# A transformer block, a state-space layer and an attention layer on one core: the transpositions between two stages moved half a block of products

## The chip, the cores and the metric

The kernel runs on one core of a Trainium2 chip. Its time is device microseconds from the start to the end of one execution. Five engines work side by side, each through its own list of instructions in a fixed order: TensorE (PE, matrix products and transpositions), VectorE (DVE), ScalarE (ACT), GpSimd (POOL) and SyncE (SP, which issues the DMAs). An instruction waits until what it reads is written, and everything behind it on its engine waits with it.

## The reference

512 tokens of width 1024 in 32-bit floats go through four stages. Each stage norms its input, scales and shifts it by vectors that come from a condition c, computes, and adds its output to the running x.

```python
def first_block(x, c, ...):
    sh1, sc1, g1, sh2, sc2, g2 = split(silu(c) @ ada_w + ada_b, 6)
    h = rms_norm(x, mix_pre_g) * (1 + sc1) + sh1
    y = hybrid_mixer(h, ...)                    # forgetting attention beside a convolution, then @ w_o
    x = x + g1 * rms_norm(y, mix_post_g)
    h = rms_norm(x, ffn_pre_g) * (1 + sc2) + sh2
    y = swiglu_ffn(h, w_ffn_in, w_ffn_out)      # silu(h @ Wg) * (h @ Wu) @ w_ffn_out
    return x + g2 * rms_norm(y, ffn_post_g)

def second_block(x, c_2, ...):
    x = x + gate * _mamba2_mixer(_modulate(x, norm_g[0], shift, scale), ...)   # ends in @ m_out_w
    kv = _modulate(x, kv_norm_g, kv_shift, kv_scale) @ kv_w
    x = x + gate * _sb_mixer(_modulate(x, norm_g[1], shift, scale), k, v, ...) # ends in @ sb_out_w
    return _rmsnorm(x, final_g)
```

## The kernel before

The 512 tokens are four blocks of 128. Every product of two 32-bit matrices is made of three products of a faster format (`mm3`, L328 to L330): each operand is split into a high part, a cast, and a low part, the rest. For weights ACT casts the high part (`whi`, L269) and DVE or POOL subtracts (`wlo`, L273). A ring of four `whi`/`wlo` buffers holds split weights, and four `raw` buffers hold what DMAs have brought; a raw buffer is loaded again when its weight is split. Some weights that are needed early go into buffers named `b` instead of the ring. Between the splits DVE also sums condition vectors from further weights that pass through the same raw buffers (L503, L505).

Three times one stage ends and the next begins: I call these places the joins. The first lies between the attention and the feed-forward part, the second between that and the mamba mixer, the third between mamba and the last attention. All three are written by `boundary`, which goes through a table of steps, `BOUNDARY`; a step is a letter and a block of tokens:

- m: the last products of the block with the output weights of the ending stage, into two PSUM buffers of 512 columns (`Out.last`, L328 to L330). For blocks 2 and 3 these are 24 products, 12 for each half of the columns.
- a: squares of the sums on ACT (L574; none at the third join) and the gate on DVE (L632)
- b, d, n: the inverse root of the mean square, six tiny instructions that alternate between DVE and ACT (L581 to L586); n does d of one block and b of the next
- c: the sum goes to x on DVE (L642; L644 at the third join), squares of x on ACT (L574)
- e: x scaled by the root into `w`: the first half on DVE (L656), the second on ACT (L658)
- r: the eight transpositions on PE, four from each half (L664), into `pa` buffers for blocks 0 and 1, `ps` buffers for blocks 2 and 3
- f: scale and shift, the first half on DVE (L674 x4), the second on ACT (L676 x4), then the high part of both halves on ACT (L680) and the low part on POOL (L681). At the third join also copies of the transposed block (L684).
- p: the first products of the next stage with that block (24 of them, L328 to L330), which read the high and low parts
- l: what comes after p (an activation or a copy out of PSUM)

The table is not the order in which an engine works. It is the order of writing; a scheduler orders each engine's instructions by their readiness as it estimates it and by a priority, which `PRIO` gives each letter (`bm` is not in it, `bp` -200, `br` -5, with other numbers in some stages). So moving a step in the table moves instructions on every engine that has to do with it.

Of the kernel before, what the change touches and what calls it, by code (L numbers as in the profile page):

```python
# [50 lines left out]
AHEAD = 11  # L51


BOUNDARY = ("m0 a0 b0 m1 m2 a1 c0 n0 e0 c1 a2 r0 n1 f0 e1 r1 m3 c2 a3 n2 p0 e2 f1 c3 n3 e3 r2 l0 f2 p1 l1 r3 p2 "
            "l2 f3 p3 l3")


class Unit:
# [71 lines left out]
class Body:  # L130
# [557 lines left out]
    def boundary(self, out, gate, norm, mod, h, first, keep=None):  # L688

        nc = self.nc  # L690
        st = [self.block(t, lambda t=t: out.pss[t], gate, norm, mod, h, keep) for t in range(NT)]
        nc.scalar.activation(self.small(), self.ones[:, 0:1], AF.Sqrt, scale=0.0)
        for s in BOUNDARY.split():
            kind, t = s[0], int(s[1])
            with self.prio("b" + kind):
                if kind == "m":
                    self.run(out.last(t))
                elif kind == "p":
                    self.run(first[t])
                elif kind == "n":  # L700

                    self.side(st[t]["d"]() if t >= 0 else [], st[t + 1]["b"]() if t + 1 < NT else [])
                elif kind == "b":
                    self.side(st[t]["b"]())
                elif kind == "d":
                    self.side(st[t]["d"]())
                elif kind == "l":
                    self.late.pop(0)()
                else:
                    st[t][kind]()  # L710
# [1019 lines left out]
```

## Time and profile before

| what | value |
|---|---|
| median of 3 runs | 1388.56 us (1387.05 to 1390.49) |
| the profiled execution's own time | 1386.6 us |
| its span, first to last instruction | 1384.9 us |
| PE busy with products | 1315.4 us, 95% of the span, 7477 instructions |
| DVE, ACT, POOL busy | 877.3 us (63%), 661.4 us (48%), 313.6 us (23%) |
| granted clock of PE, mean | 0.987 of full speed |

The profile is of one execution. Times within it count from the span's start. A row of the timeline gives the start of a group of equal instructions and how long they were busy; products are pipelined, so the steps between their starts tell their cost, not the time beside them. A number in square brackets is idle time of the engine just before, and what ended it.

### The profile page before, as it was taken

The page shows a single profiled execution, that of the slowest core. Times are in us where ns is not written, and L with a number is a line of the kernel's source. Part 1 is how long each engine was busy: PE and PEld are TensorE (multiplying, and loading weights), DVE is VectorE, ACT ScalarE, POOL GpSimd, SP SyncE. Part 2 cuts the span into 40 slices and gives each one's busy share as a digit, 9 for nine tenths or more (in the row PEclk, how much of TensorE's full clock was granted, in tenths as well). Part 3 has the DMA queues.
Part 4 walks back from the last instruction along what each step waited for, and adds up shares of the span by engine and source line. Part 5 has one row for each costly group of instructions (what it writes and reads, how often), then busy time and mean ns, then how long its engine had stood idle before and what let it go on. Part 6 is the DMA issues. An engine that isn't in the chain of part 4 may idle for free. (4 is left out here: it accounts for less than half of the span.)

```text
span 1384.9 us, 19700 instructions
## 1 busy us (share of the span) xinstructions
PE 1315.4 (95%) x7477; PEld 1024.8 (74%) x7479; DVE 877.3 (63%) x1267; ACT 661.4 (48%) x1214; POOL 313.6 (23%) x322
## 2 busy tenths in 40 slices
PE   7899899999999999999999999999899999999997
PEld 5574566777888888888768777777688787777766
DVE  7924676465455443622868889767744966777865
ACT  4433248355222223412667566667542835555543
POOL 3541323023000000000111434342400412433421
PEclk9999899999999999999999999999999999999999
DMA  9668664205376554223167455414024354232211
GB/s 301 171 181 240 184 184 136 61 16 174 115 235 213 195 187 159 91 91 111 46 183 253 137 169 162 152 52 160 32 91 137 107 168 122 76 94 75 96 42 61
DMA packets 134731, 189.06 MB, mean 137 GB/s; under 512 B 10280, under 2 KB 95556, under 8 KB 133612
## 3 DMA queue, kind: packets, MB, share of 16 engines
q1 hardware_dynamic: 134588, 187.79, 43.9%
q8 instruction: 59, 0.97, 0.3%
q14 instruction: 36, 0.29, 0.1%
q10 hardware_dynamic: 48, 0.01, 0.0%
HBM read 178.25 MB, written 3.24 MB: 131 GB/s over the span
## 5 line engine op out<-in xcount | busy, mean ns | idle before, releaser
L273 DVE TENSOR_TENSOR wlo<-raw,whi 128x1024 fp32r<-128x1024 f32 (+1 forms) x160 | 209.6, 1321 | 204.8 <-ACT whi L269 194.7
L269 ACT CAST whi<-raw 128x1024 fp32r<-128x1024 f32 (+1 forms) x177 | 182.8, 1045 | 285.9 <-PE pa L329 121.0
L329 PE MATMUL pa<-b,whi 128*128 128x512 f32 x744 | 298.6, 401 | 0.0
L328 PE MATMUL pa<-b,whi 128*128 128x512 f32 x744 | 298.4, 401 | 0.0
L330 PE MATMUL pa<-b,wlo 128*128 128x512 f32 x744 | 297.5, 400 | 0.0
L329 PE MATMUL pa<-wlo,b 128*128 128x512 f32 x424 | 167.1, 394 | 1.9 <-DVE sm L581 1.9
L328 PE MATMUL pa<-whi,b 128*128 128x512 f32 x424 | 166.4, 394 | 1.9 <-ACT b L90 1.5
L330 PE MATMUL pa<-whi,b 128*128 128x512 f32 x424 | 166.3, 394 | 0.0
L330 PEld LDWEIGHTS pa<-b,wlo 128*128 128x128 f32 x744 | 140.7, 189 | 31.9 <-issue 2.1
L505 DVE SCALAR_TENSOR_TENSOR acc<-raw,c,acc 128x1024 f32<-128x1024 f32 x84 | 118.5, 1411 | 71.6 <-DMA raw<-in_ada_w_dram 46.5
L328 PEld LDWEIGHTS pa<-b,whi 128*128 128x128 f32 x744 | 140.6, 189 | 31.3 <-issue 4.9
L329 PEld LDWEIGHTS pa<-b,whi 128*128 128x128 f32 x744 | 140.7, 189 | 29.6 <-issue 0.8
L681 POOL TENSOR_TENSOR b<-w,b 128x512 fp32r<-128x512 f32 x24 | 36.7, 1546 | 469.1 <-DVE sm L586 288.0
L328 PEld LDWEIGHTS pa<-whi,b 128*128 128x128 f32 x424 | 80.0, 189 | 19.4 <-issue 1.8
L329 PEld LDWEIGHTS pa<-wlo,b 128*128 128x128 f32 x424 | 79.9, 188 | 19.4 <-DVE wlo L273 2.7
L330 PEld LDWEIGHTS pa<-whi,b 128*128 128x128 f32 x424 | 79.9, 189 | 17.3 <-issue 0.6
L1452 DVE TENSOR_TENSOR_SCAN w<-w,own 128x512 f32<-128x512 f32 (+3 forms) x64 | 64.1, 1046 | 15.2 <-ACT w L1449 15.2
L1454 POOL TENSOR_TENSOR w<-w,w 128x511 f32<-128x511 f32 (+3 forms) x64 | 67.7, 1063 | 22.1 <-DVE w L1452 21.2
L328 PE MATMUL ps<-whi,b 128*128 128x512 f32 x184 | 72.3, 393 | 0.0
L329 PE MATMUL ps<-wlo,b 128*128 128x512 f32 x184 | 72.1, 392 | 0.0
L330 PE MATMUL ps<-whi,b 128*128 128x512 f32 x184 | 72.0, 391 | 0.0
L273 POOL TENSOR_TENSOR wlo<-raw,whi 128x1024 fp32r<-128x1024 f32 (+1 forms) x17 | 41.3, 2432 | 72.9 <-ACT whi L269 65.9
(356 smaller groups left out, 2179.7 us busy)
## 6 DMA issues: line engine op xcount, KB each, us to landing
raw<-in_ada_w_dram SPq DMA_DIRECT2D x80, 512.0 KB
raw<-in_w_ffn_in_dram SPq DMA_DIRECT2D x44, 512.0 KB
raw<-in_m_in_w_dram SPq DMA_DIRECT2D x40, 512.0 KB
raw<-in_w_ffn_out_dram SPq DMA_DIRECT2D x22, 512.0 KB
b<-in_ada_w_dram SPq DMA_DIRECT2D x16, 512.0 KB
raw<-in_kv_ada_w_dram SPq DMA_DIRECT2D x16, 512.0 KB
b<-cumd SPq DMA_DIRECT2D x8, 1024.0 KB
raw<-in_m_out_w_dram SPq DMA_DIRECT2D x16, 512.0 KB
```

The source lines that it names most:

```text
L269: nc.scalar.copy(hi[:, :n], u.raw)
L273: eng.tensor_tensor(lo[:, :n], u.raw, hi[:, :n].bitcast(F32), ALU.subtract)
L328: mm(ps, lhsT=lh, rhs=rh, start=first, stop=False)
L329: mm(ps, lhsT=lh, rhs=rl, start=False, stop=False)
L330: mm(ps, lhsT=ll, rhs=rh, start=False, stop=last)
L505: nc.vector.scalar_tensor_tensor(acc, raw, ck, acc, ALU.mult, ALU.add)
L681: nc.gpsimd.tensor_tensor(lo, y[i], hi.bitcast(F32), ALU.subtract)
L1452: nc.vector.tensor_tensor_scan(R[:, 0:N][:, ::-1], R[:, 0:N][:, ::-1], self.own[:, S - N : S][:, ::-1], 0.0, ALU.mult, ALU.max)
L1454: nc.gpsimd.tensor_tensor(pr_[:, : N - 1], pr_[:, : N - 1], R[:, 1:N], ALU.mult)
```

## The change

The table gets two new letters. h is the first half of an m step's products (the first 512 columns), q the first half of a p step's; a later m or p of the same block does what is left. Block 0's transpositions r0 stood before all of block 3's last products m3 and now stand behind their first half (h3); r1 stood before m3 and now stands behind it; r2 stood before p1 and now stands behind its first half (q1). r3 stays. The function keeps the list of products that is left of a block.

```diff
-BOUNDARY = ("m0 a0 b0 m1 m2 a1 c0 n0 e0 c1 a2 r0 n1 f0 e1 r1 m3 c2 a3 n2 p0 e2 f1 c3 n3 e3 r2 l0 f2 p1 l1 r3 p2 "
-            "l2 f3 p3 l3")
+BOUNDARY = ("m0 a0 b0 m1 m2 a1 c0 n0 e0 c1 a2 h3 r0 n1 f0 e1 m3 r1 c2 a3 n2 p0 e2 f1 c3 n3 e3 q1 r2 l0 f2 p1 l1 r3 "
+            "p2 l2 f3 p3 l3")
...
+        last = {}
         for s in BOUNDARY.split():
             kind, t = s[0], int(s[1])
-            with self.prio("b" + kind):
-                if kind == "m":
-                    self.run(out.last(t))
-                elif kind == "p":
-                    self.run(first[t])
+            with self.prio("b" + {"h": "m", "q": "p"}.get(kind, kind)):
+                if kind in "hm":
+                    if t not in last:
+                        last[t] = out.last(t)
+                    l = last[t]
+                    self.run([l.pop(0) for _ in range(len(l) // 2 if kind == "h" else len(l))])
+                elif kind in "qp":
+                    l = first[t]
+                    self.run([l.pop(0) for _ in range(len(l) // 2 if kind == "q" else len(l))])
```

Three places show what the scheduler makes of it. On PE at the third join, the kernel before has the last of block 0's first products (into `pa_9281`), then one product of block 1 (`pa_9380`), then the transpositions of block 2 (from `w_9312` and `w_9314`):

```order
L330 MATMUL pa_9281<-whi_9234,b_9060 128x512
L328 MATMUL pa_9380<-b_9024,b_9057 128x512
L664 MATMUL ps_9354<-ident,w_9312 128x128 x4
L664 MATMUL ps_9359<-ident,w_9314 128x128 x4
L329 MATMUL pa_9380<-b_9024,b_9057 128x512
```

In the changed kernel the last product of m3 (into `ps_8709`) is followed by the transpositions of block 1 (from `w_9208` and `w_9210`), those of block 2, and only then by block 0's first products (`pa_9281`):

```order
L330 MATMUL ps_8709<-whi_9012,b_9018 128x512
L664 MATMUL pa_9246<-ident,w_9208 128x128 x4
L664 MATMUL pa_9251<-ident,w_9210 128x128 x4
L664 MATMUL ps_9370<-ident,w_9312 128x128 x4
L664 MATMUL ps_9375<-ident,w_9314 128x128 x4
L328 MATMUL pa_9281<-b_9024,b_9057 128x512
```

So r1 moved from the first products of m3 to its end, and r2 from behind p0 to ahead of it. On ACT at the same join the kernel before casts block 0 (from `w_9143` and `w_9145`) before the four weight casts:

```order
L676 ACTIVATE w_9145<-pa_9164,Sk,Gk 128x128
L680 CAST b_9057<-w_9143 128x4x128
L676 ACTIVATE w_9198<-pa_9205,Sk,Gk 128x128
L680 CAST b_9058<-w_9145 128x4x128
L676 ACTIVATE w_9198<-pa_9205,Sk,Gk 128x128
L684 COPY b_9061<-pa_9159 128x4x128
L269 CAST whi_9225<-raw_9007 128x1024
```

In the changed kernel the weight casts, the rest of the modulations of blocks 0 and 1 (`w_9145`, `w_9210`) and the scaling of block 2 (`w_9314`) stand ahead of that cast:

```order
L676 ACTIVATE w_9145<-pa_9176,Sk,Gk 128x128 x2
L269 CAST whi_9215<-raw_9007 128x1024
L269 CAST whi_9224<-raw_9016 128x1024
L269 CAST whi_9233<-raw_9027 128x1024
L269 CAST whi_9288<-raw_9219 128x1024
L574 ACTIVATE junk_9333,sm_9330<-x 128x512
L676 ACTIVATE w_9145<-pa_9176,Sk,Gk 128x128 x2
L676 ACTIVATE w_9210<-pa_9251,Sk,Gk 128x128 x4
L658 ACTIVATE w_9314<-x,sm_9268 128x512
L574 ACTIVATE junk_9336,sm_9331<-x 128x512
L680 CAST b_9057<-w_9143 128x4x128
```

The cast of block 0's high part moved down by ten rows. On ACT at the first join the kernel before scales block 1 (L658 into `w_2749`) between the two casts of block 0 (`w_2679`, `w_2681`), and squares x after that:

```order
L676 ACTIVATE w_2681<-pa_2706,S_1742,G_1432 128x128 x2
L680 CAST b_2556<-w_2679 128x4x128
L658 ACTIVATE w_2749<-x,sm_2711 128x512
L680 CAST b_2557<-w_2681 128x4x128
L574 ACTIVATE junk_2810,sm_2807<-x 128x512
L676 ACTIVATE w_2749<-pa_2756,S_1742,G_1432 128x128
```

In the changed kernel two weight casts, four squarings and both casts of block 0 come between its modulations and the scaling of block 1 (here into `w_2761`):

```order
L676 ACTIVATE w_2681<-pa_2718,S_1742,G_1432 128x128 x4
L269 CAST whi_2766<-raw_2067 128x1024
L574 ACTIVATE junk_2810,sm_2807<-x 128x512
L269 CAST whi_2775<-raw_2200 128x1024
L574 ACTIVATE junk_2813,sm_2808<-x 128x512
L680 CAST b_2556<-w_2679 128x4x128
L574 ACTIVATE junk_2816,sm_2815<-ps_2530 128x512
L680 CAST b_2557<-w_2681 128x4x128
L574 ACTIVATE junk_2821,sm_2820<-ps_2531 128x512
L582 ACTIVATE sm_2828<-sm_2808,sm_2826 128x1
L582 ACTIVATE sm_2834<-sm_2820,sm_2832 128x1
L658 ACTIVATE w_2761<-x,sm_2723 128x512
```

Block 1's scaling, which its transpositions on PE read, moved behind the squares of block 2's x and block 3's sums.

## Rows read from the trace of the kernel before

**Rows 1.** Busy time by engine in four stretches: start:end, length, engines, clock, DMA.
```profile
286.00:332.00 46.00, 40.98 (x183) 31.84 (x183) 36.95 (x81) 34.53 (x79) 17.50 (x10) 0.96 0.27 92
332.00:660.00 328.00, 328.00 (x1700) 270.02 (x1699) 146.03 (x149) 88.85 (x108) 4.78 (x2) 1.00 0.48 156
660.00:724.00 64.00, 58.68 (x291) 44.68 (x291) 49.25 (x109) 43.41 (x92) 10.88 (x8) 1.00 0.36 107
...
1062.00:1106.00 44.00, 42.70 (x203) 34.84 (x203) 37.91 (x72) 29.45 (x64) 13.19 (x8) 1.00 0.39 124
```

**Rows 2.** Waits of PE over the span: total us, times, longest us.
```profile
PE ps L664 <- DVE w L656: 4.8, 4, 2.1
```

**Rows 3.** Timeline of PE at the third join: start us, us, instruction.
```profile
1076.33 1.04 PE L664 MATMUL pa<-ident,w 128*128 128x128 f32 x8
...
1083.78 0.39 PE L328 MATMUL pa<-b,b 128*128 128x512 f32 x1
...
1088.99 0.39 PE L330 MATMUL pa<-whi,b 128*128 128x512 f32 x1
...
1090.12 1.10 PE L664 MATMUL ps<-ident,w 128*128 128x128 f32 x8 [0.51 <-DVE w L656]
...
1096.32 1.03 PE L664 MATMUL ps<-ident,w 128*128 128x128 f32 x8
1097.11 0.48 PE L328 MATMUL pa<-b,b 128*128 128x512 f32 x1
...
1098.61 0.50 PE L330 MATMUL pa<-b,b 128*128 128x512 f32 x1 [0.79 <-POOL b L681]
```

**Rows 4.** Timeline of ACT, DVE and POOL at the third join.
```profile
1077.44 0.79 ACT L676 ACTIVATE w<-pa,Sk,Gk 128x128 f32<-128x128 f32 x2
...
1079.97 0.61 ACT L680 CAST b<-w 128x512 fp32r<-128x512 f32 x1
...
1082.15 3.92 ACT L269 CAST whi<-raw 128x1024 fp32r<-128x1024 f32 x4
1085.95 0.65 ACT L574 ACTIVATE junk<-x 128x512 bf16<-128x512 f32 x1
...
1088.77 0.76 ACT L658 ACTIVATE w<-x,sm 128x512 f32<-128x512 f32 x1
...
1084.01 4.62 DVE L273 TENSOR_TENSOR wlo<-raw,whi 128x1024 fp32r<-128x1024 f32 x4
...
1089.15 0.91 DVE L656 TENSOR_SCALAR w<-x,sm 128x512 f32<-128x512 f32 x1
...
1080.66 2.57 POOL L681 TENSOR_TENSOR b<-w,b 128x512 fp32r<-128x512 f32 x2 [82.69 <-ACT b L680]
```

**Rows 5.** Timeline of PE at the first join.
```profile
303.34 0.39 PE L328 MATMUL pa<-b,b 128*128 128x512 f32 x1
...
310.50 0.66 PE L664 MATMUL ps<-ident,w 128*128 128x128 f32 x4 [1.02 <-DVE w L656]
...
323.84 0.40 PE L328 MATMUL pa<-b,b 128*128 128x512 f32 x1
```

**Rows 6.** Timeline of ACT and DVE at the first join.
```profile
299.94 0.75 ACT L658 ACTIVATE w<-x,sm 128x512 f32<-128x512 f32 x1
...
300.19 3.49 DVE L642 SCALAR_TENSOR_TENSOR x<-w,sm,x 128x512 f32<-128x512 f32 x2
...
323.10 1.28 ACT L1079 ACT_TABLE_LOAD   x1
```

**Rows 7.** Busy time and clock in two stretches of the first join, columns as in rows 1.
```profile
306.00:311.00 5.00, 1.95 (x9) 0.99 (x9) 4.89 (x14) 3.98 (x9) 3.36 (x3) 1.00 0.32 105
311.00:316.00 5.00, 5.00 (x17) 3.52 (x16) 5.00 (x7) 2.75 (x6) 2.68 (x2) 0.66 0.35 108
```

**Rows 8.** Timeline of ACT and PE at the second join.
```profile
677.17 0.64 ACT L680 CAST b<-w 128x512 fp32r<-128x512 f32 x1
...
679.50 0.66 PE L664 MATMUL pa<-ident,w 128*128 128x128 f32 x4 [1.18 <-DVE w L656]
```

## The prediction

> **What bounds the kernel now.** I read the stretches first, then the waits of TensorE (PE), then the three joins instruction by instruction. In the stretch of the second stage PE is busy for all of its 328.00 us, and in the three joins around and behind it PE is short of the window by 5.0, 5.3 and 1.3 us, while VectorE (DVE) and ScalarE (ACT) are nearly as full there as PE [rows 1]. So PE sets the time. A delay of PE at the first join is passed on whole, because the stage behind it has no idle time that could swallow it. The join is a chain that goes back and forth: PE's sums are squared on ACT, scaled on DVE, transposed on PE, modulated on DVE and ACT, cast on ACT (the high part, L680), subtracted on GpSimd (POOL; the low part, L681), and only then can the next stage's products of that block start. The transpositions wait for the scaling L656 for 4.8 us in the "ps" buffers [rows 2], and once for 1.18 us in a "pa" buffer [rows 8].
>
> I call the transpositions of block t rt, the last products of a block mt, and the next stage's first products of a block pt, as the table does.
>
> **The change part by part.** Nothing is computed more or less: the same 24 products and 8 transpositions per block. What can change is who is late. Each product takes 0.2265 us: 24 of them start from 1083.78 to 1088.99, 23 steps [rows 3]. Eight transpositions take 0.8 us (1096.32 to 1097.11) [rows 3].
>
> *Third join (mamba to the attention).* Before, r2 stands behind the 24 products p0, and these cover it: it starts at 1090.12 after 0.51 us of waiting [rows 3]. In the new order r2 stands ahead of p0. "Half a block later" thus holds for r0 and r1 only; r2, ordered behind half of p1 in the table, comes 25 products earlier on PE, ahead of products whose casts stand late. With m3 done, nothing is left on PE to cover it. The next question is when p0 can begin, which needs block 0's high part, L680 on ACT. Before, that cast ran at 1079.97, ahead of the four weight casts L269 [rows 4]. Now it stands behind them, behind six of the eight modulations L676 and behind block 2's L658. Worked out: r0 starts 12 products later than 1076.33, at 1079.05, and ends at 1079.85 [rows 3]. Then ACT does two L676 (0.8), four L269 (3.8 to the next start), one L574 (0.65), six L676 at 0.4 (2.4), L658 (0.76), L574 (0.65) and L680 (0.61), all from [rows 4]: 9.7 us, so the high part is there at 1089.5, where p0 began at 1083.78 before. DVE is no earlier: its four L273 take 4.62 us [rows 4] and now follow the start of block 0's modulations, with block 2's scaling behind them, so r2 itself runs at about 1088. POOL's low part takes 1.3 us (2.57 for two) [rows 4], so the third product of p0 starts at 1090.8. From there 21 of p0, 24 of p1 and 3 of p2, 48 x 0.2265 = 10.9, and r3's 0.8 come to 1102.5 for the third product of p2. Before it was at 1098.61, and its own wait of 0.79 for the low part [rows 3] is in that number; that wait goes. The loss is 3.9 us. Behind the waiting r2 stand p0, p1 and all that follows, so every engine of the last stage moves with it. If each of the 14 ACT instructions overlaps its neighbour by 0.1 us it is 2.7.
>
> PE would be idle from about 1083.4 to 1088 there. A stretch like it lies in the first join: in 306 to 311 PE was busy for 1.95 of 5 us, and in the 5 us behind it the granted clock was 0.66 [rows 7], partly at the 1.2 GHz level; 5 us at 0.66 do the work of 3.3, so the price is 1.7 us. That is the upper end for this term, zero the lower; I take 1.0, since the idle stretch here is emptier but r2 and two products lie within it. Third join: +4.9, from +2.7 to +6.5 (3.9 + 1.7, and 0.9 for DVE and POOL hindering each other, as where L656 takes 0.91 [rows 4]).
>
> The Trainium skill, page "TensorE: Matmul & The Clock Gate", section "Part 1: The HAM clock gate", says that the halved clock is the state an idle array falls back to and activity releases. By that rule the 1.7 us would be paid in full in the third join; by the rows alone, which show one fall, it is open.
>
> *First join (attention to feed-forward).* r0 lies 8 products later, r1 nine: behind all of m3, directly ahead of p0. Its second operand, L658 on ACT, ran at 299.94 before [rows 6], ahead of four squarings L574. Now it stands behind four of them and behind two weight casts L269 that came much later before. r0's end follows from p0's old start, 303.34 [rows 5]: less r1 (0.8) and the 15 products between (3.4) it is 299.1. Then ACT: four L676 1.6, two L269 2.0, four L574 2.6, two L680 1.2, L658 0.75 = 8.2, so r1 is complete at 307.7 and p0 starts 4.3 us later than before. Against that, the old order lost time after p0's start: from 303.34 to p2's first product at 323.84 it took 20.5 us [rows 5] for work of 48 x 0.2265 + 16 transpositions (1.6) = 12.5. If nothing waits any more, p2 starts at 307.6 + 12.5 = 320.1, a gain of 3.7; if the same 20.5 us are needed, at 328.1, a loss of 4.3. I take +2.5, nearer the latter: e2 and e3 still hang on DVE, where a pair of L642 that meets POOL takes 3.49 us [rows 6], and the table load of 1.28 us [rows 6] that stood behind block 2's modulations on ACT now stands ahead of them, on the way to p2's low part. The clock's fall is in the old 20.5 us as well.
>
> *Second join (feed-forward to mamba).* r1 comes five products later and so loses its wait of 1.18 us [rows 8]: that is the lower end, -1.2. But the high part of block 0, cast at 677.17 directly behind its modulations [rows 8], now stands behind L658, two L269 and two L574 (0.75 + 2.0 + 1.3 = 4.0), with r0 12 products later. r0 ends at about 676.5 (679.50 less the wait, seven products and nothing else), four L676 1.6, those 4.0 and the cast 0.6: 682.7, where p0 could start at 679.50 + 0.8 + 1.1 = 681.4 before. That is +1.3, and twice that if the later low parts carry it on: I take +1, from -1.2 to +3.
>
> Elsewhere the rows on the engines keep their order but for some places in the stages behind, which move with PE; I cost them at nothing, since PE's products hide them.
>
> Sum: 2.5 + 1 + 4.9 = +8.4. The profiled execution's own time was 1386.6 us (span 1384.9); it becomes 1395.0. The median of the runs shown is 1388.56, 2.0 above the profiled one, so I forecast **1397.0 us**.
>
> **The rivals.**
> *The waits at the transpositions go and nothing takes their place.* PE would win 4.8 [rows 2] and 1.18 [rows 8], 6.0 us, giving 1382.6. For it: those waits are real, and half a block of products (12 x 0.2265 = 2.7 us) is longer than the longest of them, 2.1 [rows 2]. It decides if the high part of block 0 is cast before PE is through with m3. Against it: on ACT it is queued behind the weight casts in all three joins.
> *Nothing changes.* A join lasts as long as its work on DVE and ACT (37.0 and 34.5 us of 46 in the first [rows 1]), and PE only idles elsewhere: 1388.6. For it: the old order had idle time of 5 us in both of the first two joins. Against it: in the third PE had only 1.3 us of it, so a gap of 4 us there is new.
> *The clock falls at all three joins.* 1.7 us in the second, another 1.7 in the first beyond the old one, and 0.7 more in the third: +4.1 on the forecast, 1401.1. Against it: only [rows 7] shows a fall, and waits behind it hide part of one.
>
> **How the numbers follow.** Forecast 0.65, clock 0.12, nothing changes 0.16, waits go 0.07. Some 0.3% (4.2 us) is about what a measurement of this kernel can tell from no change. The forecast's own range, 1391 to 1402, lies beyond it but for its lowest tenth; with the clock's case that gives slower 0.74, same 0.19, faster 0.07. The range of 8 in 10 reaches down into the case of no change, 1389, and up beyond the clock's, 1403.
>
> **What the changed profile would show.** Right: in the third join a gap of 4 us or more on PE ahead of r2, put down to L656 or L658, and p0 starting some 6 us later than before, behind L680; no wait at r3. In the first join p0 some 4 us later, behind r1, and fewer waits after it. In the second p0 waiting for L680. Wrong: p0 of the third join following m3 without a gap, or a total wait of PE in the three windows that is smaller than before. If the third join loses its 4 us and the first gains as much, the sum fails at the first join's +2.5.

## The result, and the profile after

The changed kernel takes 1405.40 us (median of 4 runs, 1400.84 to 1408.28) beside 1387.80 us before: a ratio of 1.0114, 95% interval 1.0086 to 1.0143 (the two medians by themselves give 1.0127). The forecast of 1397.0 us had the sign and half of the size; the time lies outside the range of 1389 to 1403. The profiled execution took 1404.15 us with a span of 1402.4 us, 17.5 us longer than before.

I lay the two traces beside each other at instructions that both have. Up to the end of the first join the new one is 1.2 us late, 0.2 of it older than the join: the join cost 1.0. The second stage adds 0.1. At the first transposition of `xs` in the mamba stage (L1279 before, 763.22; L1284 after, 765.78) it is 2.6 us late, so the second join cost 1.3. From there to the first transposition of the fourth group's output (1002.81 and 1014.07) it loses **8.7 us more**, in a stage that the change does not touch. The third join costs 7.1, and 0.8 comes back behind it.

Such marks are compared by their distance from an earlier one. Executions already differ ahead of the first join: in the twelve profiled kernels that keep the old table there, its first transposition comes between 293.26 and 296.54 us (294.39 in the kernel before).

The same stretches as in [rows 1], the third join's moved by the 11 us that the kernel is late there:

```profile
286.00:332.00 46.00, 40.47 (x179) 32.28 (x178) 35.28 (x82) 32.40 (x77) 17.19 (x10) 0.89 0.34 103
332.00:660.00 328.00, 328.00 (x1701) 269.90 (x1700) 143.90 (x148) 88.89 (x108) 4.79 (x2) 1.00 0.49 154
660.00:724.00 64.00, 58.13 (x282) 43.80 (x281) 43.46 (x103) 42.03 (x88) 13.37 (x8) 1.00 0.33 96
1073.00:1117.00 44.00, 37.46 (x173) 30.80 (x172) 33.31 (x66) 23.76 (x53) 9.62 (x6) 0.92 0.39 125
```

The third join is the one that changes: PE is busy for 37.5 of 44 us, where [rows 1] had 42.7, at a clock of 0.92. Its rows on PE, which answer to [rows 3]:

```profile
1093.97 1.04 PE L664 MATMUL pa<-ident,w 128*128 128x128 f32 x8
1099.07 1.15 PE L664 MATMUL ps<-ident,w 128*128 128x128 f32 x8 [4.06 <-DVE w L656]
1102.70 0.80 PE L328 MATMUL pa<-b,b 128*128 128x512 f32 x1 [2.48 <-ACT b L684]
...
1107.21 0.39 PE L330 MATMUL pa<-b,b 128*128 128x512 f32 x1
...
1116.96 0.39 PE L330 MATMUL pa<-b,b 128*128 128x512 f32 x1
```

ACT there, which answers to [rows 4]:

```profile
1091.41 0.81 ACT L676 ACTIVATE w<-pa,Sk,Gk 128x128 f32<-128x128 f32 x2 [0.31 <-PE pa L664]
1092.11 3.89 ACT L269 CAST whi<-raw 128x1024 fp32r<-128x1024 f32 x4
...
1096.53 2.19 ACT L676 ACTIVATE w<-pa,Sk,Gk 128x128 f32<-128x128 f32 x6
1098.58 0.74 ACT L658 ACTIVATE w<-x,sm 128x512 f32<-128x512 f32 x1
...
1101.04 1.12 ACT L680 CAST b<-w 128x512 fp32r<-128x512 f32 x2
1102.07 0.58 ACT L684 COPY b<-pa 128x512 f32<-128x512 f32 x1
```

PE has r1, then r2 after 4.06 us of waiting, then p0 after 2.48 more. From 1092.11 on ACT does four casts of weights, six modulations and a scaling before the casts that p0 needs. p0 itself starts right behind the copy L684, which reads a `pa` buffer. p0's twelfth product starts 4.51 us behind its first, where 11 steps of 0.2265 us are 2.49: the granted clock fell behind the idle stretch, as the two stretches around p0's start show.

```profile
1097.00:1102.00 5.00, 1.15 (x8) 0.86 (x8) 4.91 (x14) 4.62 (x12) 0.98 (x1) 0.80 0.98 327
1102.00:1107.00 5.00, 4.30 (x11) 3.42 (x12) 5.00 (x7) 4.43 (x11) 5.00 (x4) 0.52 0.42 144
```

In the first join, which answers to [rows 5], the two halves of r1 wait, the clock falls, and yet p2 starts only 1.2 us later than before:

```profile
304.58 1.07 PE L664 MATMUL pa<-ident,w 128*128 128x128 f32 x4 [2.25 <-DVE w L656]
308.93 1.12 PE L664 MATMUL pa<-ident,w 128*128 128x128 f32 x4 [3.29 <-ACT w L658]
309.70 0.78 PE L328 MATMUL pa<-b,b 128*128 128x512 f32 x1
...
325.04 0.40 PE L328 MATMUL pa<-b,b 128*128 128x512 f32 x1
```

Now the stage that the prediction left out. The next two fences cut it in three, from the first transposition of `xs` to that of the first, the second and the fourth group's output; columns as in [rows 1]. The kernel before:

```profile
763.22:810.99 47.77, 44.68 (x313) 34.62 (x311) 43.05 (x68) 24.93 (x47) 18.33 (x14) 1.00 0.50 163
810.99:880.17 69.18, 66.37 (x471) 53.02 (x471) 59.38 (x86) 44.15 (x84) 25.43 (x23) 1.00 0.45 136
880.17:1002.81 122.64, 112.45 (x793) 89.29 (x793) 86.88 (x132) 82.31 (x158) 50.81 (x46) 1.00 0.28 100
```

The kernel after:

```profile
765.78:820.52 54.74, 48.31 (x310) 37.15 (x308) 44.23 (x71) 33.48 (x61) 17.59 (x14) 0.91 0.45 149
820.52:891.46 70.94, 67.16 (x474) 53.46 (x474) 58.73 (x86) 44.36 (x85) 25.83 (x23) 1.00 0.45 132
891.46:1014.07 122.61, 112.37 (x794) 89.29 (x793) 86.87 (x132) 82.33 (x158) 50.84 (x46) 1.00 0.30 101
```

PE does the same work in the first third (310 and 313 products; some records are missing from a trace) and takes 7.0 us more for it: 3.3 of idle time (54.74 less 48.31 against 47.77 less 44.68) and 3.6 of slower products. ACT is busy for 8.6 us more: some exponentials that lay ahead of the first mark now lie behind it, and loads of function tables stand between them. Over the whole trace there are 50 such loads where there were 44. The two lines that changed most, in the grouping by line (count, busy us, mean ns), before:

```profile
L1270 ACT ACT_TABLE_LOAD x10 | 12.8, 1283 | 0.2
L1147 ACT ACT_TABLE_LOAD x7 | 9.0, 1283 | 2.8 <-DVE w L1145 2.7
```

And after:

```profile
L1275 ACT ACT_TABLE_LOAD x13 | 16.7, 1283 | 3.1 <-DMA b<-cumd 3.0
L1152 ACT ACT_TABLE_LOAD x11 | 14.1, 1283 | 3.4 <-DVE w L1150 3.3
```

The exponentials of the decays (L1270, now L1275) and the Silus of the convolutions (L1147, now L1152) use different tables, and in the new order ACT goes back and forth between them. On PE 74 of the projections' products, 15 more than before, stand between the first transposition of `xs` and the first diagonal block. The first product of the group's states waits longer. PE before:

```profile
767.67 0.50 PE L328 MATMUL ps<-w,b 128*128 128x512 f32 x1 [0.38 <-ACT w L1243]
...
769.78 0.50 PE L329 MATMUL ps<-w,b 128*128 128x512 f32 x1 [1.28 <-POOL w L1244]
...
781.45 0.74 PE L1296 MATMUL ps<-w,b 128*64 128x64 f32 x18
```

PE after:

```profile
771.23 0.50 PE L328 MATMUL ps<-w,b 128*128 128x512 f32 x1 [1.36 <-ACT w L1248]
...
773.16 0.80 PE L329 MATMUL ps<-w,b 128*128 128x512 f32 x1 [1.21 <-POOL w L1249]
...
791.15 1.04 PE L1301 MATMUL ps<-w,b 128*64 128x64 f32 x28
```

The clock falls behind these waits, towards the 1.2 GHz level:

```profile
770.00:775.00 5.00, 2.56 (x8) 1.89 (x9) 4.76 (x6) 2.74 (x7) 2.37 (x2) 0.73 0.57 190
775.00:780.00 5.00, 5.00 (x15) 3.92 (x14) 2.56 (x4) 2.65 (x7) 1.28 (x1) 0.59 0.30 111
```

### The profile page after: what moved, and what is told of

Its sections match the earlier page's. It is cut to its first block, busy times and chain, and to the rows that moved or that the text cites. A ratio compares the mean times of both kernels' runs of the same rounds, so it can differ in the third digit from the quotient of the medians.

```text
span 1402.4 us, 19703 instructions
## 1 busy us (share of the span) xinstructions
PE 1322.4 (94%) x7479; PEld 1030.7 (73%) x7479; DVE 867.8 (62%) x1267; ACT 671.7 (48%) x1220; POOL 315.4 (22%) x322
## 5 line engine op out<-in xcount | busy, mean ns | idle before, releaser
L273 DVE TENSOR_TENSOR wlo<-raw,whi 128x1024 fp32r<-128x1024 f32 (+1 forms) x160 | 205.9, 1297 | 217.7 <-ACT whi L269 207.7
L269 ACT CAST whi<-raw 128x1024 fp32r<-128x1024 f32 (+1 forms) x177 | 183.1, 1045 | 293.5 <-PE pa L329 122.2
L330 PEld LDWEIGHTS pa<-whi,b 128*128 128x128 f32 x424 | 79.8, 188 | 17.5 <-issue 0.6
```

The costliest lines, as they stand in the source:

```text
L269: nc.scalar.copy(hi[:, :n], u.raw)
L273: eng.tensor_tensor(lo[:, :n], u.raw, hi[:, :n].bitcast(F32), ALU.subtract)
L330: mm(ps, lhsT=ll, rhs=rh, start=False, stop=last)
```

## The experiments

Below, a time is given as its ratio to the kernel before on the same chip, with its 95% interval, and in us of some 1390. In the kernels with one table for each join, `o` is the old table and `n` the new one:

```diff
+BOUNDARY = {"fox": n, "ffn": o, "mamba": o}      # t_first; the ending stage names the join
-        for s in BOUNDARY.split():
+        for s in BOUNDARY[self.stage].split():
```

**One join at a time.** t_first:

> The new table at the first join alone (mixer to feed-forward), the old one at the other two. Theory A (what the two traces suggest: each join pays its own price, and the rest of the 17 us comes from the state-space stage, whose instructions on ACT come out in another order with the new table at the second join): the first join costs +1.0 us, as PE's third block of m2 to p2 shows in the traces, nothing else is lost, so +1 us on the kernel before, within 0.3 %. Theory P (the prediction's terms): +2.5 us. Theory D (any delay ahead of the state-space stage upsets it, whatever table stands where): +1 at the join and about +8 in the state-space stage, +9 us.

Measured: 1.0003 (0.9989 to 1.0017), +0.4 us. P's +2.5 lies just outside the interval (-1.5 to +2.4 us) and D's +9 far outside: the first join costs nothing that the times can tell, and a join with another order does not by itself upset the mamba stage (240.5 us from first to last mark, 239.6 before).

t_second:

> The new table at the second join alone (feed-forward to state-space), the old one at the other two. Theory A: +1.3 us at the join and about +8.5 us in the state-space stage, between its 55th and 85th us, where ACT's loads of function tables multiply (52 in the whole program against 44 before) and the first group's last exponential ends some 20 us later: +10 us on the kernel before. Theory P (the prediction's terms, the stage behind the join moves with PE): +1 us. Theory D (any delay ahead upsets the stage): as A here, +9 us.

Measured: 1.0049 (1.0035 to 1.0062), **+6.8 us**. P's +1 is out, and D is out by t_first. Theory A holds in kind, but its +10 lies above the interval (+4.9 to +8.6). The mamba stage's first third, in which the clock held until 808 us this time and the idle time was the larger:

```profile
763.60:816.82 53.22, 45.56 (x309) 35.28 (x308) 46.83 (x73) 33.80 (x63) 17.30 (x14) 0.97 0.48 156
```

PE is idle for 7.7 us there (3.1 before). `xs` starts at 763.60, 0.4 us later than before, in an execution that was 0.7 us ahead at the first join (its first transposition at 293.71): the second join costs 1.1, and the larger part is lost behind it.

t_third:

> The new table at the third join alone (state-space to attention), the old one at the other two. Theory A: +7.0 us at the join, as the changed kernel's trace showed it, less 0.8 in the last stage: +6 us on the kernel before; the clock at the join falls as in the changed kernel (0.93 in the 44 us around it). Theory P: +4.9 us. Theory E (the third join's 7 us were so dear only because the state-space stage ahead had another order, its transfers and splits too): +3 us or less.

Measured: 1.0037 (1.0022 to 1.0051), +5.1 us, with a clock of 0.88 in 1062 to 1106. P's +4.9 and A's +6 both lie within the interval (+3.1 to +7.1), E's +3 or less just below it.

t_first_third:

> The new table at the first and the third join, the old one at the second. Theory A (prices add up, and the state-space stage keeps an order with few table loads, 42 in the program): +1.0 + 6 = +7 us. Theory P: +7.4 us, which tells nothing apart by itself; the state-space stage does: A and P have it as long as before within 1 us, theory D has it 8 us longer, +15 us in all.

Measured: 1.0050 (1.0033 to 1.0067), +7.0 us, and 241.1 us from mark to mark in the mamba stage. Prices add up, D is out again.

**The third join in parts.** t_third_early has the table with `h3 r0 ... m3 r1` and the old end, t_third_late the old beginning and `q1 r2`, both at the third join alone.

> At the third join alone the early half of the change: the third block of m2 is cut in half, r0 stands between its halves and r1 behind it, but p0 is not cut and r2 keeps its place behind p1's tokens in the table; the other joins as in the kernel before. In PE's program r2's transpositions still come to stand right behind r1's, ahead of p0. Theory F (the third join's loss is r2 standing ahead of p0 without anything to do in between, and p0's late splits; both come from the early half): as with the whole new table there, +5 to +6 us. Theory G (the loss comes from q1 and r2, the late half): 0 to +1 us.

Measured: 1.0040 (1.0025 to 1.0056), +5.6 us: theory F. The early half alone brings r2 ahead of p0 and has the whole price.

> At the third join alone the late half of the change: p1's block is cut in half and r2 stands between its halves; r0 and r1 stand as before. In PE's program p0 comes ahead of r2. Theory F: no loss, and the 0.5 us that r2 waited at 1090 us in the kernel before may go: 0 to -1 us. Theory G: +5 to +6 us.

Measured: 1.0016 (1.0002 to 1.0030), +2.2 us: neither G nor a gain. F's 0 lies just outside the interval; what these 2 us are I did not find.

That r2 stands ahead of p0 could be the cause, or only a neighbour of it. third_r2_back adds to t_third:

```diff
+                elif s == "r2" and self.stage == "mamba":
+                    n = len(self.instructions())
+                    st[t][kind]()
+                    for i in self.instructions()[n:]:
+                        if "PE" in str(i.engine):
+                            self.order(i, p0)      # the last product of p0
```

> The new table at the third join alone (1.0037 of the kernel before), and one order added on PE: r2's transpositions stand behind the products of p0 and p1. Nothing is changed on ACT's order of the splits: four casts of weights still stand between r1's transpositions and the second half of what makes p0's tokens. Theory R (PE loses the time in r2, which waits 4.3 us for DVE with p0 queued behind it): the loss goes, 0 to +1.5 us on the kernel before. Theory S (p0 itself is late: its second half waits for ACT's and DVE's splits of weights, some 8 us, and r2's wait only lies in the shadow of that): PE stands still in front of p0 instead, for 6 us or more, and the loss stays, +4 to +6 us.

Measured: 1.0064 (1.0045 to 1.0083), +8.9 us: no gain at all, and more than theory S said. PE's only wait there has moved to p0:

```profile
1093.24 0.80 PE L331 MATMUL pa<-b,b 128*128 128x512 f32 x1 [7.80 <-ACT b L687]
```

r1 starts at 1084.39 and p0 8.85 us behind it; in t_third, with r2 between, it was 9.00 (1084.88 and 1093.88). r2's wait of 4.33 us there lay in the shadow of what p0 waits for. Theory S. PE's idle time is longer than t_third's (7.80 us against 4.33 and 1.66), since r2 is no longer done within it; that is a part of the 3.8 us more, the rest is not shown.

third_f_up is t_third with `"mamba.bf": 200` for -400.

> The new table at the third join alone, and the priority of that join's step f (shift, scale and split of the tokens) raised from -400 to 200, nothing else: on ACT the splits of weights then stand behind the first two blocks' steps but for two casts, and PE's program has p0 and p1 ahead of r2. Theory S: p0 starts some 4 us earlier than with the table alone, so +0 to +2 us on the kernel before. Theory R by itself gives the same, since r2 stands behind p0; the kernel with r2 alone held back tells the two apart. Rival T (the splits, now later, make PE's products wait for their weights): the gap moves from p0's front into p0 or p1, on whi or wlo, and the loss stays, +4 us or more.

Measured: 1.0010 (0.9997 to 1.0023), +1.4 us: 3.7 of the 5.1 us are gone. Only two of the four casts of weights still stand between r1 and p0's second half:

```profile
1085.85 1.04 PE L667 MATMUL pa<-ident,w 128*128 128x128 f32 x8
1088.54 0.50 PE L331 MATMUL pa<-b,b 128*128 128x512 f32 x1 [1.64 <-ACT b L687]
```

The clock read 1.00 from 1084 to 1104 us, where t_third had 0.50 and 0.51 in the two stretches of 5 us from 1089 on: what is won holds the clock's price as well. So the late place of block 0's step f on ACT, behind the casts of weights, together with r0 and r1 lying half a block later, is the third join's cause. before_f_up, the same priority with the old table:

> The kernel before with the priority of the third join's step f raised from -400 to 200 and nothing else. PE's two small waits there (0.5 us ahead of r2, 0.8 us for p2's tokens) may go: theory S, 0 to -1.5 us. Rival T (weights come late): +1 to +3 us, with a wait on whi or wlo behind r1.

Measured: 1.0012 (0.9997 to 1.0027). No gain. Beside it third_f_up, at 1.0010, has nothing left of the new table's price at that join.

**The mamba stage.** after_decay_up is the changed kernel with `"decay": -300` for -860, before_decay_up the kernel before with `"decay": 500`.

> The changed kernel with the priority of the state-space stage's exponentials raised (decay -860 to -300) and nothing else. In PE's program the first diagonal product then stands behind 59 of the projections' products, as in the kernel before, and not behind 74; ACT's loads of tables among the first group's exponentials are 9 (5 before, 11 in the changed kernel). Theory O (the state-space stage lost its 8 us because the first diagonal block, from which DVE's and GpSimd's chain of the group starts, was put 15 products later): the stage from its first transposition of xs to the fourth group's is as long as before within 2 us, and the whole is some 7 us faster than the changed kernel, +8 to +10 us on the kernel before. Theory L (the loads of tables cost it, which hold ACT and with it the exponentials): most of the loss stays, +13 to +16 us. Theory K (the clock that fell in that stage cost it): the loss goes only if the granted clock at 770 to 780 us is 1.00.

Measured: 1.0081 (1.0063 to 1.0099), +11.3 us. The stage takes 244.9 us (248.3 in the changed kernel, 239.6 before). The first third is mended to 50.1 us, the second takes 72.1 (70.9). The stage is not within O's 2 us, and the time lies between O and L, its interval (+8.8 to +13.8) touching both. The clock was 0.70 from 770 to 775 us and 0.96 from 775 to 780, so K's condition was not met.

> The kernel before with the priority of the exponentials raised much further (decay -860 to 500): the first group's exponentials stand in one piece with 1 load of tables among them, 32 loads in the whole program against 44, and the first diagonal product stands behind 31 of the projections' products. Theory L: 12 loads less of 1.28 us each on ACT, some of them beside PE's work, so -4 us or more on the kernel before. Theory O: the chain of the group starts some 28 products (6 us) earlier, but the products left behind it must be done too: -3 to 0 us. If ACT's other work is pushed behind the exponentials (the splits of weights that PE waits for), slower: +3 us or more.

Measured: 1.0097 (1.0079 to 1.0115), **+13.5 us** with twelve loads fewer: L and O are out, and the last case of the three, work pushed behind the exponentials, came true. PE waits for 8.04 us at one place; the rest of the loss is not traced here:

```profile
841.81 0.80 PE L328 MATMUL ps<-w,b 128*128 128x512 f32 x1 [8.04 <-ACT b L1251]
```

ACT does 32 exponentials in one piece there, and the cast that PE waits for (L1251) stands behind them:

```profile
830.47 9.47 ACT L1270 ACTIVATE b<-b,w 128x128 f32<-128x128 f32 x32
839.83 0.61 ACT L1243 CAST w<-w 128x512 fp32r<-128x512 f32 x1
840.34 1.05 ACT L269 CAST whi<-raw 128x1024 fp32r<-128x1024 f32 x1
841.29 0.47 ACT L1251 CAST b<-ps 128x384 fp32r<-128x384 f32 x1
```

The Trainium skill, page "ScalarE: Activation LUTs", section "Table sets: the hidden batching unit", advises to do all the work of one table set before going to the next. Here the loads go down and the time goes up, because other engines wait for what is queued behind the batch: the measurement decides.

second_silu_back is t_second with the Silus held back:

```diff
+            n = len(silus)
             self.run(main[g + 1], s + e)
+            if g == 0:
+                for i in silus[n:]:
+                    self.order(i, exps[31])        # the first group's last exponential
```

> The new table at the second join alone (its time was 1.0049 of the kernel before), and one order added on ACT: the Silus of the second group's convolutions that are issued beside the first group's exponentials stand behind the last of these. 7 loads of tables among the 32 exponentials (5 in the kernel before, 11 without the added order), the first diagonal block behind 64 products (59 and 74). Theory L (ACT's order costs the state-space stage its time: loads and Silus between the exponentials make the last of them late, and the chain of the group starts late): the last exponential ends within 8 us of the first transposition of xs, where it ended 22 us behind it, the first diagonal block starts at most 20 us behind that transposition (23.2 without the added order, 18.2 to 20.7 in kernels with the old table there), and the whole is +1 to +3 us on the kernel before. Theory M (ACT's order is only a sign; the loss is made elsewhere in the stage): still +6 to +8 us. If holding the Silus back starves PE of the second group's B and C, slower still: +10 us.

Measured: 1.0035 (1.0019 to 1.0051), +4.9 us. The last exponential starts within 15 us of the first transposition of `xs`, some 7 us earlier in its stage than in t_second, and still the first diagonal block starts 22.5 us behind it (23.2). ACT's last four exponentials:

```profile
779.53 1.28 ACT L1279 ACTIVATE b<-b,w 128x128 f32<-128x128 f32 x4
```

PE's first state and first diagonal block:

```profile
771.87 0.50 PE L331 MATMUL ps<-w,b 128*128 128x512 f32 x1 [2.24 <-ACT w L1252]
...
788.00 1.15 PE L1305 MATMUL ps<-w,b 128*64 128x64 f32 x32
```

Theory L's condition was met only in half (the last exponential was to end within 8 us and ends within 15.3), and the interval (+2.6 to +7.1) reaches from L's +3 to M's +6. The trace speaks against L: the last exponential ends 7.2 us ahead of the diagonal block, and PE comes to that block without a wait, through the 64 products that its own order has ahead of it. The wait for the first state is as long as without the added order (2.24 us, and 2.28 in t_second).

Was the stage's order the cause at all, or the join? The halves of the table at the second join alone answer it, since they leave the stage its old order.

> At the second join alone the early half of the change (m2's third block cut, r0 between its halves, r1 behind it; p0 not cut, r2's place kept), the old table elsewhere. The state-space stage then keeps its old order: 59 products ahead of the first diagonal block, 5 loads of tables among the first group's exponentials. Theory N (the second join's loss is that stage's other order): the stage from its first transposition of xs to the last group's is 239 to 242 us, as in the kernels with the old table, and the whole 0 to +1.5 us on the kernel before. Theory J (the loss is made at the join, by r1 behind the block, and only shows later): +4 to +7 us.

Measured: 0.9993 (0.9980 to 1.0007). Theory N: the stage takes 241.4 us. Its first third:

```profile
762.72:811.80 49.08, 44.85 (x312) 34.54 (x311) 44.47 (x69) 25.50 (x49) 17.56 (x14) 1.00 0.50 162
```

> At the second join alone the late half of the change (p1's block cut, r2 between its halves; r0 and r1 as before), the old table elsewhere. The state-space stage again keeps its old order (59 products, 5 loads). Theory N: 0 to +1 us. Theory J, in its other form (the loss comes from r2 and the cut block): +4 to +7 us.

Measured: 1.0021 (1.0008 to 1.0035), +2.9 us: above N, below J. In its profiled execution, 2.1 us longer than its median, the stage took 245.6 us with its old order, its first third 52.2 at a clock of 0.93, with 4.7 us of idle time: a fall of the clock does not need the new order. Taken over all profiled runs, PE is idle in that third for 3.1 to 4.7 us in the eleven kernels that have the stage in its old order, and for 6.4 to 7.7 us in the four that have it in the new one with nothing mended. The whole stage takes 239.6 to 243.3 us in ten of the eleven (245.6 in second_late) and 247.5 to 248.4 in the four. The kernel before has the shortest of all, so 8.7 is an upper value for the loss; from the middle of the one group to that of the other it is some 7.

One length hardly varies: from the first product of the first diagonal block to the first transposition of the group's output it is 29.3 to 30.0 us in every profiled kernel but before_decay_up. So the first third is as long as PE takes to reach that block, and what lies ahead of it can be priced from the rows. In t_second:

```profile
769.97 0.50 PE L331 MATMUL ps<-w,b 128*128 128x512 f32 x1 [2.28 <-ACT w L1251]
...
771.57 0.50 PE L332 MATMUL ps<-w,b 128*128 128x512 f32 x1 [0.89 <-POOL w L1252]
...
786.78 0.92 PE L1304 MATMUL ps<-w,b 128*64 128x64 f32 x24
```

PE reaches the block 23.2 us behind the first transposition of `xs`, where it took 18.2 before. Of these 5.0 us the 15 products are 3.4 (at 0.2265) and the longer waits 1.5 (2.28 and 0.89 against 0.38 and 1.28). In the changed kernel it takes 25.4 us, 7.1 more: 3.4 for the products, 0.9 for the waits, and the 2.8 that are left come with the low clock of 770 to 780 us.

**The sum.** after_again, and after_f_up, the changed kernel with `"mamba.bf": 200`:

> The changed kernel once more, unchanged, timed beside the others. If the parts add up: +0.4 +6.8 +5.1 = +12.3 us, 1.0089 of the kernel before. If they make each other dearer (a later third join meeting other transfers, more stretches at the low clock): +16 us, 1.0114, as at first.

Measured: 1.0104 (1.0084 to 1.0123), +14.5 us. The three parts multiplied give 1.0089, within this interval and the first one: it agrees with the sum of the parts, with at most a few us beyond. The mamba stage took 248.4 us again.

> The changed kernel with the priority of the third join's step f raised from -400 to 200 and nothing else: the state-space stage keeps its new order (74 products, 11 loads), the third join has p0 and p1 ahead of r2 and its tokens ahead of all but two casts of weights. If the parts add up, the third join's +5.1 us fall to +1.4 and the whole is 4 us below after_again. If the later state-space stage had already taken up the third join's wait, nothing is gained.

Measured: 1.0079 (1.0063 to 1.0095), +11.0 us, 3.5 below after_again, as the parts say, though the two intervals overlap.

No kernel here beats the one before; the nearest, second_early, is the same within 0.2%.

## Why the prediction was wrong

- **"Elsewhere the rows on the engines keep their order but for some places in the stages behind, which move with PE; I cost them at nothing."** This step failed, and with it the sum. The "some places" were 15 products ahead of the first diagonal block and ACT's exponentials among Silus. They did not move with PE: the stage took 8.7 us longer in the trace. With the new table at the second join alone the kernel is 6.8 us slower, with the early half of it, which leaves that order, the same, and with the late half, which leaves it too, 2.9. PE's products did not hide it, because the group's chain starts only when PE reaches that block: the rows give 3.4 us to the 15 products, 0.9 to 1.5 to the waits and up to 2.8 to the clock. No run separates these three cleanly: with 59 products again and 9 loads 5.3 of 8.7 us stayed, with the Silus held back and 64 products 5.6 of 7.9 (245.2 and 247.5 against 239.6 before).
- **Third join, +4.9.** Mechanism and size are right: 5.1 by itself. r2 waits 4.06 us for L656, and r3 has no wait, as said. The four L269 are in the way of p0, and putting two of them behind its step f mends it. That r2 stands ahead of p0, which the prediction tells first, is not the cause: holding it back gained nothing. In the changed kernel's trace the join cost 7.1. The clock's price was 2.0 and not 1.0, and p0 stood behind the copy L684, which I left out: its third product was worked out for 1090.8, 1102.1 with the 11.3 us of lateness, and would have come at 1103.2 at full clock, 1.1 us later. The Trainium skill, page "TensorE: Matmul & The Clock Gate", section "Part 1: The HAM clock gate", has an idle array fall back to the halved clock; the trace agrees, with 0.52 in the stretch behind the idle one, and by that rule the price of 1.7 would have been taken in full.
- **First join, +2.5.** p0 is 6.4 us late, behind r1, as said (4.3 worked out). The difference is ACT's wait of 1.93 us for DVE at L582, which stands ahead of L658 in the order shown and is not in my sum:

```profile
307.79 0.48 ACT L582 ACTIVATE sm<-sm,sm 128x1 f32<-128x1 f32 x2 [1.93 <-DVE sm L581]
```

Most of the waits behind p0 go: from p0 to p2 it takes 15.3 us and not 20.5. The loss is 1.0 in the trace and 0.4 (-1.5 to +2.4) by itself. I had taken a value near the upper end of -3.7 to +4.3; it lay between, and the 2 us too many covered a part of what the mamba stage lost.

- **Second join, +1.** 1.3 in the trace at `xs`, 1.1 in t_second, and p0 waits for L680, as said:

```profile
683.86 0.50 PE L328 MATMUL pa<-b,b 128*128 128x512 f32 x1 [2.22 <-ACT b L680]
```

- **The rivals.** That the clock falls at more joins (1401.1) comes nearest to the time, for half of the wrong reason: it fell in the first and the third join (0.89 and 0.92) but not in the second (1.00 from 660 to 724 us), and in the mamba stage (0.91 in its first third), which no rival named. The interval of the ratio leaves no room for the other two, no change and a gain.

## What to carry to other kernels

Where a scheduler orders the engines, a move of twenty instructions can reorder a stage that the diff doesn't touch: compare the order of the whole program, count what differs in each stage (products ahead of the first link of a chain, loads of tables), and give each such place a price with both signs, rather than none. When several instructions wait in a row, take away the first wait alone before you blame it: a longer one may stand behind it. Cut a table-like change at each place where it acts; each piece then has its own price, and their sum tells whether anything is left unexplained.

## What the runs showed of the hardware

A load of ACT's function table took 1283 ns each time (44 loads in the kernel before, 50 in the changed one), and ACT's next instruction can follow it at once: the load at 323.10 [rows 6] is followed at 324.39. The length of PE's waits alone does not tell whether the clock falls: at the same place of the mamba stage, behind 2.6 us of waiting it fell in the changed kernel (0.73, then 0.59), and behind 3.2 us it held in t_second (1.00 until 808 us). What decides it, these runs do not show.
